# The SSD branch in two halves of its channels over four column tiles, and at most one side task begun per step

## The chip, the cores and the metric

The kernel runs on one core of a Trainium2 chip. The metric is the device time of one execution in microseconds (us); the times are medians of several executions.

## The reference, cut to what matters

One layer of a hybrid encoder for two requests of 256 tokens each (512 tokens in all), model width 1024, fp32:

```
x = x + 0.5 * swiglu(rms_norm(x), ffn1)
u = rms_norm(x);  q_na, k_na, v_na, q_mem, z, xbc, dt, gates = split(u @ w_in)
o_na  = neighborhood_attention(q_na, k_na, v_na)         # 16 heads of 64
o_ssd = grouped_rms_norm(ssd(xbc, dt) * silu(z), 8)      # 2048 channels, 8 groups of 256
o_mem = memory_attention(q_mem, mem)                     # 4 heads of 256
merged = sigmoid(g_na) * (o_na @ w_br_na) + sigmoid(g_ssd) * (o_ssd @ w_br_ssd) + sigmoid(g_mem) * (o_mem @ w_br_mem)
x = x + merged @ w_out
x = x + 0.5 * swiglu(rms_norm(x), ffn2)
```

The product `o_ssd @ w_br_ssd` has 2048 input channels (16 tiles of 128) and 1024 output channels (8 column tiles of 128).

## The kernel before

**Arithmetic.** Every product is made of three fp32r matmuls: each operand x is split into a high part (a cast to fp32r) and a low part (x minus the high part), and high x high, high x low and low x high are summed. So a weight tile `wr` of 128 x 1024 costs a cast `wh` on ScalarE (line 320) and a subtraction `wl` on VectorE (line 234), and an activation tile costs the same pair (`split_tile`: `osh`/`osl` for the SSD output, `mhh`/`mhl` for the merged one).

**The plan.** `make_plan` writes the whole layer as one list of units: the first FFN, the memory's keys and values, the projections for the attentions, the gates and branches of the memory attention, then for each of 8 SSD groups four convolution units and two z units with a gate or branch unit of the neighbourhood attention between them, then the 8 gate units of the SSD branch (`gate`, `ssd`, j), its 8 branch units (`br`, `ssd`, j), 8 units of the output projection (`wo`), and the second FFN. A unit of a gate has 8 x 3 matmuls of 512 columns; a unit of the SSD branch has 16 x 3, from two weight tiles of 8 channel tiles each, into one PSUM bank.

**Order around a unit.** `run` calls the unit's `do_` function (its matmuls), then `evacuate` (the evacuation of the unit before), then `step` (one step of the side tasks; after a gate of the SSD branch a second one). The evacuation of gate j is a tanh on ScalarE from the bank to a tile `tg`; that of branch j multiplies `tg` with the bank and adds it to `merged[j]`, which is then split.

**Side tasks.** What stands beside the matrix products (norms, attention, scans) is written as Python generators, put into a queue by `later` and advanced one yield per `step`. `step` advances every active task once, in order, and then begins tasks from the head of the queue; a task begins only when those it needs are done and not in the slot in which it was queued. Up to `width` tasks are active (3; 4 from the first gate of the SSD branch on), and the loop gives as many chances to begin one as `width`. `require` runs steps until given tasks are done. The ones that matter here:

- `na(p)`, p = 0 to 7 (`t_na`, 6 steps): a pair of heads of the neighbourhood attention. Step 1 issues 8 loads `nv<-scr_v` and the bias `bi<-in_strip` on SP and transposes the queries; step 2 transposes the keys and adds a mask to the bias on VectorE; step 3 makes the scores `ns` in two banks, adds the bias to them (`nt`), takes maxima and exponentials; then come the normalisation, the transposes and the output.
- `ssd(g)`, g = 0 to 7 (`t_ssd`, 14 steps): the scan of group g, with rows `rw<-scr_r` loaded on SP, matmuls `y`, and at the end the norm: a `sum` on PE, a chain of small VectorE operations, a diagonal `dg`, and `R` on PE, which spreads the norm. Groups 0 to 5 are parked in memory (`scr_o`, `scr_n`); 6 and 7 stay in SBUF (tiles `cv`).
- `os(g)` (`t_os`, one step): two tiles of the branch's input each. For g < 6 the norm (`rw<-scr_n`) and the tiles (`or<-scr_o`) are loaded on SP; each is scaled and split into `osh` and `osl`. `os(0)` to `os(3)` are queued at gate 0, `os(4)` to `os(7)` at the start of the branch, which requires all eight.

**Buffers.** Activations come from two pools, `pg` (54 tiles: u, cv, tg, mg, or, osh, osl, x, ...) and `pt` (21 tiles for temporaries: rw, e, nv, bi, ...). Weight tiles have a ring of 9, their split parts one of 3. PSUM has 5 banks for units (`m`, `q`, `ac`) and 3 for side tasks and the down projection. The order in which an engine gets its instructions is made by a scheduler at compile time: it goes by program order as a priority and by its own estimate of when inputs and buffers are there, so the queues differ from program order.

Of the kernel before, what the change touches and what calls it, by code (L numbers as in the profile page):

```python
# [10 lines left out]
ALU = mybir.AluOpType  # L11
# [5 lines left out]
KD = 8  # L17
# [24 lines left out]
def add_item(*args, **kw):  # L42
    ITEMS.append(Item(*args, **kw))
    return len(ITEMS) - 1


def plain(mat, k0, nk, col, m):
    n = f"c{len(ITEMS)}"
    return add_item(n, nk, m, [(n, (mat, k0, nk, col, m))])


def seven(p, key, block, nh):

    out = []
    for h in range(nh):
        n = lambda b: f"gu{key}.{h}.{b}"  # L60
        blk = lambda b: block(int(b[1]) - 1, int(b[2]) - 1, h)
        loads, src, sums = {1: (["B11"], "B11", []), 2: (["B21"], "B21", []), 5: (["B12"], "B11", [("B11", "B12")]),
                            6: (["B22"], "B11", [("B11", "B22")]), 3: ([], "B22", []), 7: ([], "B12", [("B12", "B22")]),
                            4: (["B21."], "B11", [("B11", "B21.")])}[p]
        _, _, nk, _, m = blk("B11")
        it = add_item(n(src), nk, m, [(n(b), blk(b)) for b in loads], [tuple(n(b) for b in t) for t in sums])
        out.append(("gu", (*key, p, h, nh), [it]))
    return out


def make_plan():

    s = []

    def a(kind, key, mat, col, ks=((0, 8),), m=128):
        s.append((kind, key, [plain(mat, k0, nk, col, m) for k0, nk in ks]))

    def quad(kind, q, mat, col):
        for c in range(4):
            s.append((kind, (q, c), [plain(mat, 2 * c, 2, col, 512)]))  # L80

    def ffn(f):

        before = None
        for ci, (c0, w) in enumerate(CBLOCKS + ((DFF, 0),)):
            n, down = w // 256, list(range(4)) if before else []

            def next_down():
                if down:
                    mp = down.pop(0)
                    s.append(("d", (f, ci - 1, mp), [plain(f + "_w_down", before[0], before[1], 256 * mp, 256)]))

            def part(p, ci=ci, c0=c0, w=w, n=n):
                s.extend(seven(p, (f, ci), lambda i, j, h: (f + ("_w_up", "_w_gate")[j], 4 * i + 4 // n * h, 4 // n, c0, w), n))

            if f == "ffn1" and ci == 0:
                for j, mat in enumerate(("_w_up", "_w_gate")):  # L100
                    for c in range(4):
                        s.append(("pl", (f, j, c), [plain(f + mat, 2 * c, 2, c0, w)]))
            else:
                for p in PRODUCTS if w else ():
                    if p == 4 and ci == 0:
                        rest = part
                        continue
                    part(p)
                    if p == 1 and ci == 1 and f == "ffn2":
                        rest(4)  # L110
                    if p in ((5, 6, 3, 7) if n == 2 else (5, 3, 7, 4)):
                        next_down()
            for _ in range(4):
                next_down()
            before = (c0 // 128, w // 128)

    def gate(br, j):
        a("gate", (br, j), "w_in", COL_G + 1024 * ("na", "ssd", "mem").index(br) + 128 * j)

    def branch(br, j):  # L120
        a("br", (br, j), "w_br_" + br, 128 * j, ks=((0, 8), (8, 8)) if br == "ssd" else ((0, 8),))

    ffn("ffn1")
    quad("km", 0, "w_mem_kv", 0)
    quad("km", 1, "w_mem_kv", 512)
    quad("vm", 0, "w_mem_kv", 1024)
    quad("vm", 1, "w_mem_kv", 1536)
    a("dt", 0, "w_in", COL_DT, m=64)
    quad("qm", 0, "w_in", COL_QM)
    quad("qm", 1, "w_in", COL_QM + 512)  # L130
    quad("v", 0, "w_in", COL_V)
    quad("v", 1, "w_in", COL_V + 512)
    for hf in range(2):
        quad("q", hf, "w_in", 512 * hf)
        quad("k", hf, "w_in", 1024 + 512 * hf)
    for j in range(8):
        gate("mem", j)
        branch("mem", j)
    light = [(f, j) for j in range(8) for f in (gate, branch)]
    for g in range(8):  # L140
        for i, (ct, col) in enumerate(((16 + g, COL_B + 128 * g), (24 + g, COL_C + 128 * g), (2 * g, COL_X + 256 * g),
                                       (2 * g + 1, COL_X + 256 * g + 128))):
            a("conv", (g, ct), "w_in", col)
            if i in (2, 3) and light:
                f, j = light.pop(0)
                f("na", j)
        a("z", (g, 0), "w_in", COL_Z + 256 * g)
        a("z", (g, 1), "w_in", COL_Z + 256 * g + 128)
    for j in range(8):
        gate("ssd", j)  # L150
    for j in range(8):
        branch("ssd", j)
    for m in (0, 4, 1, 5, 2, 6, 3, 7):
        a("wo", m, "w_out", m * 128)
    ffn("ffn2")
    return s


PLAN = make_plan()
CHUNKS = list(dict.fromkeys(c for it in ITEMS for _, c in it.loads))  # L160
OFFS = dict(zip(CHUNKS, np.concatenate([[0], np.cumsum([128 * nk * m for _, _, nk, _, m in CHUNKS])]).tolist()))
# [17 lines left out]
KEEP, EARLY, PG, LEND = 6, 4, 54, 4  # L179
# [3 lines left out]
class Layer:  # L183
# [145 lines left out]

    def step(self):  # L330

        for item in list(self.active) + [None] * self.width:
            if item is None:
                if len(self.active) >= self.width or not self.queue:
                    return
                _, _, need, born = self.queue[0]
                if born == self.n_slot or not all(k in self.done for k in need):
                    return
                item = self.queue.popleft()
                self.active.append(item)  # L340
            try:
                next(item[1])
            except StopIteration:
                self.done.add(item[0])
                self.active.remove(item)
# [692 lines left out]
    def pre_br(self, key):  # L1038
        br, j = key
        if j:  # L1040
            return
        if br == "mem":
            self.require(*[("am", h, b) for h in range(4) for b in range(2)])
            self.xo = [self.o.pop(("om", k)) for k in range(8)]
        elif br == "na":
            self.require(*[("na", p) for p in range(8)])
            self.xo = [self.o.pop(("on", k)) for k in range(8)]
        else:
            self.evacuate()
            self.u = None  # L1050
            for g in range(EARLY, 8):
                self.later(("os", g), self.t_os(g), (("ssd", g),))
            self.require(*[("os", g) for g in range(8)])
            self.xo = [self.os[k] for k in range(16)]

    def do_br(self, key, cis):
        br, j = key
        if key == ("ssd", 4):
            self.x = []
            for k in range(KD):  # L1060
                t = self.g(p="x2")
                self.nc.sync.dma_start(out=t, in_=self.scr_x[k])
                self.x.append(t)
        ps = self.unit(cis, self.xo)

        def evac():
            t = self.o.pop(("gate", br, j))
            if br == "mem":
                self.merged[j] = self.g(p="mg")
                self.stt(self.merged[j], t, 1.0, ps, ALU.add, ALU.mult)  # L1070
                return
            self.stt(t, t, 1.0, ps, ALU.add, ALU.mult)
            m = self.merged[j]
            self.tt(m, m, t, ALU.add)
            if key == ("na", 7):
                self.lent = 0
            if br == "ssd":
                self.merged[j] = self.split_tile(m, "mh")
        return evac

    def pre_wo(self, m):
# [335 lines left out]
```

## Time and profile before

| | |
|---|---|
| time, median of 3 runs | 1767.65 us (1766.73 to 1767.78) |
| the profiled execution | 1768.09 us, its span 1766.3 us |
| PE busy | 1741.1 us (99%) |
| VectorE (DVE) busy | 1232.2 us (70%) |
| ScalarE (ACT) busy | 847.3 us (48%) |
| mean granted TensorE clock | 0.994 |
| SSD branch, first to last matmul | about 1285.5 to 1373 us of the span |

PE is the TensorE, PEld its weight loads, SP the engine whose queue issues the DMAs. The granted clock is 1.00 at the higher of TensorE's two levels (2.4 GHz) and 0.50 at the lower (1.2 GHz). A matmul's duration overlaps the next one's; the distance of two starts tells what one costs.

### The profile page before, as it was taken

Reading aid. Unit: us, or ns where it says so; the run is one execution under the profiler, and the core shown is the slowest. Engines: PE = TensorE matmul, PEld = TensorE weight load, DVE = VectorE, ACT = ScalarE, POOL = GpSimd, SP = SyncE. Lnnn points to the kernel's source line nnn. Section 1 sums busy time; section 2 is a strip of 40 time slices with the busy share of each in tenths; the row PEclk is TensorE's granted clock in tenths of the full one; section 3 lists DMA queues with packets and bytes.
Section 4 is the critical chain, followed back from the end, with each engine's and each line's share of the span. In section 5 each row is a group of like instructions: output and inputs, shape, how many; then the busy total and the mean of one; then the engine's idle time right before and its main releaser. Section 6 shows DMA issues by size and latency. Waiting matters only on the chain.

```text
span 1766.3 us, 22623 instructions
## 1 busy us (share of the span) xinstructions
PE 1741.1 (99%) x8568; PEld 1425.2 (81%) x8568; DVE 1232.2 (70%) x2056; ACT 847.3 (48%) x1515; POOL 0.7 (0%) x5
## 2 busy tenths in 40 slices
PE   9999999999999999999999999999799999999999
PEld 7888888888788878888877777777588878888887
DVE  7676776875544466735778888888653697776775
ACT  6444444553323335533666766666432464444442
POOL 0000000000000000000000000000000000000000
PEclk9999999999999999999999999999899999999999
DMA  7144324442323232333344545347344234244341
GB/s 258 62 137 144 107 96 137 158 151 86 97 74 114 78 114 66 120 96 96 119 128 130 127 141 137 116 143 188 121 130 133 83 98 140 84 145 130 96 120 48
DMA packets 79708, 209.69 MB, mean 119 GB/s; under 512 B 11120, under 2 KB 19696, under 8 KB 79600
## 3 DMA queue, kind: packets, MB, share of 16 engines
q1 hardware_dynamic: 79600, 208.26, 38.1%
q8 instruction: 67, 1.10, 0.3%
q14 instruction: 41, 0.34, 0.1%
HBM read 198.64 MB, written 9.58 MB: 118 GB/s over the span
## 4 chain that ended last, share of the span: by engine, by line
PE 95%; DVE 3%; DMA 1%; issue 0%; ACT 0%; DVEq 0%; SPq 0%; ACTq 0%
PE ac L565 20%; PE m L543 12%; PE m L544 12%; PE m L545 12%; PE q L587 5%; PE q L589 5%; PE q L588 5%; PE d L544 5%; PE d L545 5%; PE d L543 5%; PE y L1278 2%; PE hT L690 1%; PE CB L1228 1%; DVE wl L234 1%; PE amo L875 1%; PE am L847 1%
## 5 line engine op out<-in xcount | busy, mean ns | idle before, releaser
L320 ACT CAST wh<-wr 128x1024 fp32r<-128x1024 f32 (+1 forms) x357 | 371.3, 1040 | 700.6 <-PE m L544 173.0
L234 DVE TENSOR_TENSOR wl<-wr,wh 128x1024 fp32r<-128x1024 f32 (+1 forms) x357 | 431.6, 1209 | 274.8 <-ACT wh L320 269.9
L543 PE MATMUL m<-uh,wh 128*128 128x512 f32 (+1 forms) x584 | 235.1, 403 | 2.7 <-ACT tg L249 2.7
L565 PE MATMUL ac<-wh,sh 128*128 128x512 f32 (+1 forms) x616 | 229.3, 373 | 0.8 <-ACT wh L320 0.8
L544 PE MATMUL m<-ul,wh 128*128 128x512 f32 (+1 forms) x584 | 229.0, 392 | 0.0
L565 PE MATMUL ac<-wl,sh 128*128 128x512 f32 (+1 forms) x616 | 228.1, 370 | 0.7 <-DVE wl L234 0.7
L545 PE MATMUL m<-uh,wl 128*128 128x512 f32 (+1 forms) x584 | 228.7, 392 | 0.0
L565 PE MATMUL ac<-wh,sl 128*128 128x512 f32 (+1 forms) x616 | 228.1, 370 | 0.0
L544 PE MATMUL d<-hl,wh 128*128 128x512 f32 x352 | 137.3, 390 | 0.7 <-DVE hl L234 0.7
L543 PEld LDWEIGHTS m<-uh,wh 128*128 128x128 f32 (+1 forms) x584 | 109.7, 188 | 34.9 <-ACT wh L320 5.4
L543 PE MATMUL d<-hh,wh 128*128 128x512 f32 x352 | 137.4, 390 | 0.5 <-ACT hh L256 0.5
L545 PE MATMUL d<-hh,wl 128*128 128x512 f32 x352 | 137.0, 389 | 0.0
L565 PEld LDWEIGHTS ac<-wh,sh 128*128 128x128 f32 x616 | 116.0, 188 | 21.0 <-ACT wh L320 1.7
L565 PEld LDWEIGHTS ac<-wl,sh 128*128 128x128 f32 x616 | 116.1, 188 | 20.6 <-DVE wl L234 1.2
L565 PEld LDWEIGHTS ac<-wh,sl 128*128 128x128 f32 x616 | 116.1, 188 | 19.6
L545 PEld LDWEIGHTS m<-uh,wl 128*128 128x128 f32 (+1 forms) x584 | 109.6, 188 | 25.2 <-issue 0.8
L544 PEld LDWEIGHTS m<-ul,wh 128*128 128x128 f32 (+1 forms) x584 | 109.8, 188 | 22.5 <-issue 0.4
L245 DVE SCALAR_TENSOR_TENSOR x<-d,x 128x512 f32<-128x512 f32 x96 | 66.2, 690 | 75.9 <-PE d L545 75.4
L587 PE MATMUL q<-wh,uh 128*128 128x512 f32 x256 | 103.0, 402 | 0.0
L234 DVE TENSOR_TENSOR wr<-wr,wr 128x1024 f32<-128x1024 f32 x80 | 97.6, 1221 | 7.1 <-DMA wr<-in_w 6.1
L588 PE MATMUL q<-wh,ul 128*128 128x512 f32 x256 | 100.7, 393 | 0.0
L589 PE MATMUL q<-wl,uh 128*128 128x512 f32 x256 | 100.6, 393 | 0.0
(253 smaller groups left out, 2856.5 us busy)
## 6 DMA issues: line engine op xcount, KB each, us to landing
wr<-in_w SPq DMA_DIRECT2D x308, 512.0 KB
rw<-scr_r SPq DMA_DIRECT2D x64, 256.0 KB
nv<-scr_v SPq DMA_DIRECT2D x64, 64.0 KB
scr_o<-cv SPq DMA_DIRECT2D x12, 256.0 KB
or<-scr_o SPq DMA_DIRECT2D x12, 256.0 KB
wr<-in_w SPq DMA_DIRECT2D x9, 256.0 KB
x<-in_xT SPq DMA_DIRECT2D x8, 256.0 KB
mr<-in_memT SPq DMA_DIRECT2D x8, 256.0 KB
```

Of the source, the lines that this page charges most:

```text
L234: self.V.tensor_tensor(out=out, in0=a, in1=b, op=op)
L245: self.V.scalar_tensor_tensor(out=out, in0=a, scalar=s, in1=b, op0=op0, op1=op1)
L320: self.S.copy(hi[:, :n], t[:, :n])
L543: self.T.matmul(ps[:m], wh[:, kk, :], xh, start=i == 0, stop=False)
L544: self.T.matmul(ps[:m], wh[:, kk, :], xl, start=False, stop=False)
L545: self.T.matmul(ps[:m], wl[:, kk, :], xh, start=False, stop=i == n - 1)
L565: go = lambda l, r, **f: self.T.matmul(ps, l, r, skip_group_check=True, **f)
L587: self.T.matmul(self.qb[t], xh, wh[:, kk, :], start=k == 0, stop=False)
L588: self.T.matmul(self.qb[t], xl, wh[:, kk, :], start=False, stop=False)
L589: self.T.matmul(self.qb[t], xh, wl[:, kk, :], start=False, stop=k == KD - 1)
L690: self.T.transpose(ps[:, (2 * r + t) * 128:(2 * r + t + 1) * 128], o["sg", r, t][:, c * 128:(c + 1) * 128], self.ident)
L1278: T.matmul(yb[64 * hp:64 * hp + 64, b * 256:(b + 1) * 256], xt[i][:, (2 * b + st) * 128 + 64 * hp:(2 * b + st) * 128 + 64 * hp + 64], w[hp ...
```

## The change

It does two things. First, the SSD branch is no longer 8 units of 16 channel tiles but 16 units `bs` of 8: for column tiles 0 to 3 the first 8 channel tiles, then for the same four the other 8, then the same for column tiles 4 to 7. Four banks are open at once. Only `os(0)` to `os(3)` are required before the first of them, `os(4)` to `os(7)` (still queued at the start of the branch) before the first second half. x is loaded back at unit (4, 0), where it was at branch 4. Second, `step` gives one chance to begin a task instead of `width`.

```diff
     def branch(br, j):
-        a("br", (br, j), "w_br_" + br, 128 * j, ks=((0, 8), (8, 8)) if br == "ssd" else ((0, 8),))
+        a("br", (br, j), "w_br_" + br, 128 * j)
...
-    for j in range(8):
-        branch("ssd", j)
+    for j0 in (0, 4):
+        for hf in range(2):
+            for j in range(j0, j0 + 4):
+                s.append(("bs", (j, hf), [plain("w_br_ssd", 8 * hf, 8, 128 * j, 128)]))
...
     def step(self):
 
-        for item in list(self.active) + [None] * self.width:
+        for item in list(self.active) + [None]:
...
+    def do_bs(self, key, cis):
+
+        j, hf = key
+        if key == (0, 0):
+            self.evacuate()
+            self.u = self.xo = None
+            for g in range(EARLY, 8):
+                self.later(("os", g), self.t_os(g), (("ssd", g),))
+            self.bs = {}
+        if j == 0:
+            self.require(*[("os", g) for g in range(4 * hf, 4 * hf + 4)])
+        if key == (4, 0):
+            self.x = []
+            for k in range(KD):
+                t = self.g(p="x2")
+                self.nc.sync.dma_start(out=t, in_=self.scr_x[k])
+                self.x.append(t)
+        if hf == 0:
+            self.bs[j] = self.bank()
+        ps = self.bs[j]
+        ci, = cis
+        self.ahead(ci)
+        wh, wl = self.split.pop(ci)
+        for kk in range(8):
+            xh, xl = self.os[8 * hf + kk]
+            k = 8 * hf + kk
+            go = lambda l, r, **f: self.T.matmul(ps, l, r, skip_group_check=True, **f)
+            go(wh[:, kk, :], xh, start=k == 0, stop=False)
+            go(wh[:, kk, :], xl, start=False, stop=False)
+            go(wl[:, kk, :], xh, start=False, stop=k == 15)
+        if hf == 0:
+            return None
+
+        def evac():
+            t, ps, m = self.o.pop(("gate", "ssd", j)), self.bs.pop(j), self.merged[j]
+            self.stt(t, t, 1.0, ps, ALU.add, ALU.mult)
+            self.tt(m, m, t, ALU.add)
+            self.merged[j] = self.split_tile(m, "mh")
+        return evac
```

The parts of `pre_br` and `do_br` for the SSD branch, which did the same for whole units, are removed.

## Rows read from the trace of the kernel before

**Rows 1.** The page: busy time by engine, and the clock in 40 slices.

```profile
PE 1741.1 (99%) x8568; PEld 1425.2 (81%) x8568; DVE 1232.2 (70%) x2056; ACT 847.3 (48%) x1515; POOL 0.7 (0%) x5
...
PEclk9999999999999999999999999999899999999999
```

**Rows 2.** Windows: stretch, length, busy time and instructions by engine, clock, DMA.

```profile
655.00:670.00 15.00, 11.70 (x114) 9.34 (x113) 12.27 (x31) 9.78 (x45) 0.00 (x0) 0.77 0.19 62
...
1256.00:1277.00 21.00, 10.57 (x39) 8.05 (x39) 11.49 (x28) 5.96 (x10) 0.00 (x0) 0.67 0.32 101
1285.50:1373.00 87.50, 87.50 (x386) 71.79 (x385) 40.65 (x49) 25.92 (x32) 0.00 (x0) 1.00 0.41 132
```

**Rows 3.** Timeline of PE at the gates: start, duration, instruction [idle before <-releaser].

```profile
1227.02 0.95 PE L504 MATMUL sum<-consts,yq 128*128 128x1 f32 x8
...
1234.55 1.05 PE L521 MATMUL R<-dg,consts 128*128 128x128 f32 x8
...
1262.69 1.70 PE L504 MATMUL sum<-consts,yq 128*128 128x1 f32 x8 [4.10 <-DVE yq L234]
1268.06 2.05 PE L521 MATMUL R<-dg,consts 128*128 128x128 f32 x8 [3.68 <-DVE dg L512]
1272.76 0.80 PE L543 MATMUL m<-uh,wh 128*128 128x512 f32 x1 [2.65 <-ACT tg L249]
...
1276.65 0.40 PE L543 MATMUL m<-uh,wh 128*128 128x512 f32 x1
```

**Rows 4.** Timeline of ScalarE at the gates and the branch's start.

```profile
1271.59 0.62 ACT L256 CAST osh<-or 128x512 fp32r<-128x512 f32 x1 [4.68 <-DVE or L245]
1272.12 2.54 ACT L249 ACTIVATE tg<-m 128x512 f32<-128x512 f32 x5
...
1302.09 2.18 ACT L256 CAST osh<-cv 128x512 fp32r<-128x512 f32 x4
```

**Rows 5.** Timeline of VectorE at the gates and the branch.

```profile
1232.51 0.69 DVE L234 TENSOR_TENSOR osl<-or,osh 128x512 fp32r<-128x512 f32 x1
...
1236.57 1.40 DVE L245 SCALAR_TENSOR_TENSOR cv<-cv,half,R 128x512 f32<-128x512 f32 x2
...
1249.76 0.69 DVE L234 TENSOR_TENSOR osl<-or,osh 128x512 fp32r<-128x512 f32 x1
...
1302.82 2.49 DVE L234 TENSOR_TENSOR osl<-cv,osh 128x512 fp32r<-128x512 f32 x4
1308.36 0.69 DVE L245 SCALAR_TENSOR_TENSOR tg<-tg,m 128x512 f32<-128x512 f32 x1 [3.04 <-PE m L545]
...
1311.53 0.69 DVE L245 SCALAR_TENSOR_TENSOR tg<-tg,m 128x512 f32<-128x512 f32 x1
```

**Rows 6.** SP's own waits, 1180 to 1320 us: total, times, longest.

```profile
SPq L288 <- DVE wl L234: 105.0, 18, 19.0
```

**Rows 7.** Timeline of SP's queue at the attention's start.

```profile
652.80 0.33 SPq L945 DMA_DIRECT2D bi<-in_strip  x1
```

**Rows 8.** Timeline of VectorE at the attention's start.

```profile
650.20 0.76 DVE L234 TENSOR_TENSOR bi<-bi,consts 128x256 f32<-128x256 f32 x2 [4.70 <-DMA bi<-in_strip]
...
657.44 0.76 DVE L234 TENSOR_TENSOR bi<-bi,consts 128x256 f32<-128x256 f32 x2 [3.96 <-DMA bi<-in_strip]
...
659.85 1.28 DVE L245 SCALAR_TENSOR_TENSOR nt<-ns,bi 128x512 f32<-128x512 f32 x2
```

**Rows 9.** Timeline of PE in the attention.

```profile
660.59 1.72 PE L979 MATMUL ns<-kT,qbd 64*64 64x128 f32 x32 [3.13 <-DVE nt L245]
...
725.84 1.60 PE L979 MATMUL ns<-kT,qbd 64*64 64x128 f32 x32 [0.85 <-DVE on L234]
```

**Rows 10.** Timeline of SP's queue at the gates.

```profile
1233.06 0.85 SPq L1316 DMA_DIRECT2D rw<-scr_n  x2
1233.96 0.90 SPq L1202 DMA_DIRECT2D rw<-scr_r  x2
...
1262.28 1.03 SPq L1316 DMA_DIRECT2D rw<-scr_n  x2
```

More of the change, by code (lines that the diff above doesn't have):

```diff
@@ L1044, in pre_br @@
             self.xo = [self.o.pop(("om", k)) for k in range(8)]
-        elif br == "na":
+        else:
             self.require(*[("na", p) for p in range(8)])
             self.xo = [self.o.pop(("on", k)) for k in range(8)]
[L1048 to L1054, printed above, removed]
     def do_br(self, key, cis):
         br, j = key
[L1058 to L1063, printed above, removed]
         ps = self.unit(cis, self.xo)
@@ L1076, in evac @@
                 self.lent = 0
-            if br == "ssd":
-                self.merged[j] = self.split_tile(m, "mh")
+        return evac
[35 more added lines that the diff above has]
+            self.merged[j] = self.split_tile(m, "mh")
         return evac
```

## The prediction

> **What bounds the kernel now.** The page comes first: TensorE (PE) is busy 1741.1 of 1766.3 us [rows 1]. Nothing that leaves PE's work and its waits alone can shorten this kernel. So a change has at most 25.2 us of PE idle to win, plus what PE loses to a lower clock. The strip of granted clock over 40 slices dips once, in the 31st [rows 1]. The windows, taken there and at every stretch where PE is not full, show two holes: 1256 to 1277 us and 655 to 670 us [rows 2]. The rest of PE's idle is scraps of under 1 us, the start and the tail.
>
> *The hole at the gates, 14.0 us.* Idle is 21.00 - 10.57 = 10.43 us, which the timeline of PE splits into 4.10, 3.68 and 2.65 [rows 2, 3]. The mean granted clock is 0.67: after it had stood idle, PE ran at the lower of its two levels (1.2 GHz). So nine matmuls take 3.9 us (1272.76 to 1276.65) instead of 9 x 0.227 = 2.0, the eight records of the sum 1.70 instead of 0.95 and those of R 2.05 instead of 1.05 [rows 3]: 3.6 us.
>
> Who is late? The last wait says it: PE waits for the tanh of a gate (tg) on ScalarE, and five of these stand in one row at 1272.12, right behind the last cast osh of the first four SSD groups [rows 3, 4]. Eight gate units run there, and the pool of matmul banks has five. Gates 1 to 5 had filled all five, so gate 6 could not start, and PE had nothing to put between the steps of the side task ssd(7). Tanh 1 had its input long before. What it lacked was a buffer for tg. The rows show that the pool pg gives buffers out in program order: the casts osh from cv stand at 1302.09, straight behind the last one from or, though two of these four cv tiles were scaled at 1236.57 and ScalarE had idled, 4.68 us before a single cast [rows 4, 5]. In program order the tasks os(0) to os(3) all stand in the first step after gate 1, before tanh 1, and their eight tiles come 5.75 us apart: (1249.76 - 1232.51) / 3 [rows 5]. Each load stands in SP's queue behind a weight load that waits for its ring buffer, 105.0 us in all in that stretch [rows 6].
>
> *The hole in the attention, 6.7 us.* Idle is 15.00 - 11.70 = 3.3 us, and the mean clock of 0.77 costs (1 - 0.77) x 15 = 3.4 more, since PE was busy while it was low [rows 2]. Three tasks na are begun in one step, so 27 loads enter SP's queue together; the third's bias is issued at 652.80 [rows 7]. VectorE stands at the bias of the second and third for 4.70 and 3.96 us, and the first's scores, which would free the score banks for PE, are read only behind that, at 659.85 [rows 8]. PE waits 3.13 us for it [rows 9].
>
> **The change part by part.**
>
> *Halves.* Matmuls (16 units x 24 = 384, as 8 x 48), weight loads (16), evacuations (8) and their operations stay the same in number. The branch fills 87.50 us, PE is busy 87.50 of them with 386 records, 0.227 us each, at clock 1.00 [rows 2]: there is no wait to remove. The scheduler that orders each engine's queue already does here what the halves do: the first two units are evacuated at 1308.36 and 1311.53 us [rows 5], 3.2 us apart although a unit takes 48 x 0.227 = 10.9, so their first halves ran early and together. Value: 0. No gain is possible; a loss needs late tiles of os(4) to os(7). They are done at 1302.82 + 2.49 = 1305.3, which is 19.8 us after the branch starts [rows 2, 5]. Four first halves cover 4 x 5.44 = 21.8 us; without that cover PE would wait for the rest. x comes back at the same place, half way, in eight loads on SP as before; the last of them may wait for an os buffer, and nothing reads that tile before the last output tile: 0. The removed require moves os(4), os(5), os(6) behind units (1,0), (2,0), (3,0) and os(7) to the start of (0,1). But the scheduler runs ahead of the program where a buffer is free: rw of os(4) was issued at 1262.28, 23 us before its place [rows 10]. So the end stays near +20: 0.
>
> *One begin per step.* I counted the queue through by hand, from the yields of each task: in 11 steps of the kernel before, more than one task begins. Three change nothing that PE waits for: two at the start (the squares end some three steps later, still three units before they are required) and one at the start of the second FFN. Three are those of the memory attention, where PE shows no wait: 0. The one at the branch is costed above. Three of the neighbourhood attention and one at the gates are left.
>
> Attention: na(0), na(1), na(2) now begin one unit of 24 x 0.227 = 5.44 us apart. The first's scores then stand ahead of the second's bias on VectorE, and a step asks for two score banks, not six. The bias of the later tasks is still somewhat late, since SP issues as many loads, but only VectorE waits, under PE's weight tiles split ahead. Bounds: 0 (the stall stays) to 6.7. For the leftover I take a place where only two tasks had begun together: PE idle 0.85 us at 725.84 [rows 9], with some clock 1.2. **-5.5 us.**
>
> Gates: os(0) and os(1) now stand behind gate 1, os(2) and os(3) behind gate 2, so tanh 1 gets its buffer after the fourth tile (1249.76 [rows 5]), not the eighth. Its bank is free before gate 5 ends (1262.69 - 4.10 = 1258.6 [rows 3]), and gate 6 fills 24 x 0.227 = 5.44 us in which PE was idle. Tanh 2 to 5 stay behind the eighth tile at 1272, and gate 7 starts there: the wait is shorter, not gone. Bounds: 0, if the eighth tile comes one gate later as its place does, to 14.0, if the tiles come faster. For the latter speaks that rw of os(2) and os(3) no longer take temporaries ahead of ssd(7)'s rows (1233.06 before 1233.96 [rows 10]). I take the mechanism between, **-5.4 us**.
>
> Sum: 1768.09 (the profiled execution: span 1766.3 and 1.8 around it) - 5.5 - 5.4 = 1757.2. That execution lies 0.4 above the median of the runs, so **1757 us**.
>
> **The rivals.**
>
> *Both holes close.* 1767.65 - 14.0 - 6.7 - 0.9 for the scrap at 726 us = 1746. For it: ssd(7) gets its rows earlier and may end under gate 6. Against: eight tiles at 5.75 us still need 40 us from the first to the last, and gates 2 to 5 wait for them.
>
> *Only the attention gains.* The chain of os tiles ends a gate later and eats what tanh 1 gives: 1767.65 - 5.5 = 1762.
>
> *The change does nothing.* The scheduler orders by its own estimate of times; if it packs the staggered tasks together again, the waits stay: 1768, within 0.2% (3.5 us, about what can be told from no change).
>
> *Slower: os(2) and os(3) come late.* Their loads now stand behind the weight loads of gate 2 and perhaps 3, and SP has waited up to 19.0 us for one ring buffer [rows 6]. Each us that the eighth tile comes later moves gate 7. Later by 16.4 us (three gates), the gates lose 16.4 - 5.4 = 11.0, and with the attention's 5.5 the time is 1773. It decides from 10.9 us on. Against it: the tiles came at an even 5.75 us, so no single wait of SP had held them that long.
>
> *Clock lost to the banks' turns.* At 0.43 us, as the nine slow ones ran, 384 matmuls would cost 78 us more; six times nine at that level, 1.85 us each, would cost 11 and bring the time back to 1768. The trace speaks against it: on five banks, with two units interleaved, the granted clock of the branch is 1.00 [rows 2]. The Trainium skill has a rule of this kind (TensorE: Matmul & The Clock Gate, "A second HAM failure mode: psum-queue depth-cycling"): cycling through PSUM banks makes PE idle briefly between groups of matmuls, and its clock swings between the two levels. By that rule the halves, which hold four banks open at once, would lose time in the branch; the 87.50 us at full clock contradict it here.
>
> **How the numbers follow.** Both holes shrink, 1750 to 1761: 0.60. Both close, 1743 to 1750: 0.10. Only the attention gains, 1761 to 1764: 0.12. Nothing, 1764 to 1771: 0.11. Late os: 0.05. Clock: 0.02, counted as slower at its upper end. Faster is 0.60 + 0.10 + 0.12 = 0.82, same 0.11, slower 0.07. The range 1746 to 1765 holds the first and the third, half of the second and a quarter of the fourth: 0.80.
>
> **What would show it.** Attention: the scores of one task per unit, no PE idle over 1 us at 655 to 670, clock 1.00. Gates: one tg at about 1250 us, between the fourth and the fifth osh, then four or five in a row; PE's wait before gate 7, not gate 6; the stretch from the first gate to the first branch matmul shorter by 5 us. Branch: 87 us as before, PE full. I would be wrong if tanh 1 stays behind all eight casts, if a wait for osh or osl appears at the first second half, or if PE waits for a bias again.

## The result and the profile after

The changed kernel takes 1756.6 us (median of 4 runs, 1756.35 to 1756.83); the kernel before took 1767.72 us beside it (4 runs). The ratio is 0.9937, with a 95% interval of 0.9919 to 0.9954: 11 us faster, at a forecast of 1757. The span of the profiled execution fell from 1766.3 to 1754.9 us.

The page of the changed kernel, in the lines that answer to [rows 1]:

```profile
PE 1737.2 (99%) x8568; PEld 1419.9 (81%) x8568; DVE 1234.6 (70%) x2056; ACT 848.0 (48%) x1515; POOL 0.7 (0%) x5
...
PEclk9999999999999999999999999999999999999999
```

PE's work is the same 8568 matmuls, its busy time 3.9 us less, since fewer ran at the low clock. The dip of the 31st slice is gone from the strip, but a slice is 44 us long and a shorter dip can hide in one. So the windows come next. They are the stretches of [rows 2], the second and third shifted by what the kernel had gained by then:

```profile
655.00:670.00 15.00, 14.31 (x124) 11.44 (x116) 12.46 (x31) 9.51 (x36) 0.00 (x0) 1.00 0.34 109
1253.00:1274.00 21.00, 13.80 (x61) 10.92 (x60) 11.37 (x27) 6.59 (x11) 0.00 (x0) 0.84 0.36 114
1274.85:1362.40 87.55, 87.55 (x388) 72.47 (x387) 40.77 (x50) 26.53 (x33) 0.00 (x0) 1.00 0.40 130
```

In the attention PE idles 0.69 us in place of 3.3 and its granted clock is 1.00 in place of 0.77. At the gates 7.20 us of idle stay of 10.43, at a mean clock of 0.84. The branch is full at clock 1.00, as before, with four banks open at once.

The timeline of PE, with the waits of the attention and the gates, to hold against [rows 3, 9]:

```profile
657.54 0.66 PE L951 MATMUL qT<-consts,qr 128*128 128x128 f32 x4 [0.69 <-DVE nt L247]
...
1221.99 0.94 PE L506 MATMUL sum<-consts,yq 128*128 128x1 f32 x8
...
1255.72 1.02 PE L506 MATMUL sum<-consts,yq 128*128 128x1 f32 x8
...
1259.87 1.13 PE L523 MATMUL R<-dg,consts 128*128 128x128 f32 x8 [0.48 <-DVE dg L514]
1267.72 0.79 PE L545 MATMUL m<-uh,wh 128*128 128x512 f32 x1 [6.72 <-ACT tg L251]
...
1271.26 0.39 PE L547 MATMUL m<-uh,wl 128*128 128x512 f32 x1
...
1361.92 0.39 PE L545 MATMUL m<-mhh,wh 128*128 128x512 f32 x1
```

Three waits at the gates have become one of 6.72 us before gate 7 and one of 0.48. The second sum now runs in between the matmuls of gate 6, with no wait; R follows right behind them. The timeline of ScalarE says why the wait before gate 7 is there:

```profile
1244.23 0.60 ACT L258 CAST osh<-or 128x512 fp32r<-128x512 f32 x1
1246.07 0.59 ACT L251 ACTIVATE tg<-m 128x512 f32<-128x512 f32 x1
1249.19 0.62 ACT L258 CAST osh<-or 128x512 fp32r<-128x512 f32 x1 [2.53 <-DVE or L247]
...
1266.56 0.62 ACT L258 CAST osh<-or 128x512 fp32r<-128x512 f32 x1 [3.74 <-DVE or L247]
1267.08 2.54 ACT L251 ACTIVATE tg<-m 128x512 f32<-128x512 f32 x5
```

One tanh, that of gate 1, stands between the fourth and the fifth cast; the next five stand in one row behind the eighth.

**Where the time came from.** The same instruction in both traces tells it: one at the first FFN's end, the branch's first matmul and the first product behind the branch. Timelines of PE, first of the kernel before, then of the changed one (its `m<-mhh` stands above):

```profile
350.71 0.50 PE L543 MATMUL d<-hh,wh 128*128 128x512 f32 x1 [0.24 <-ACT hh L256]
...
1285.50 0.39 PE L543 MATMUL m<-osh,wh 128*128 128x512 f32 x1
...
1372.99 0.39 PE L543 MATMUL m<-mhh,wh 128*128 128x512 f32 x1
```

```profile
351.15 0.50 PE L545 MATMUL d<-hh,wh 128*128 128x512 f32 x1 [0.24 <-ACT hh L258]
...
1274.88 0.39 PE L1094 MATMUL m<-osh,wh 128*128 128x512 f32 x1
```

At the first FFN's end, 350.71 before and 351.15 after, the changed kernel is 0.44 us late. At the first `sum` above, before the gates' holes, it is 1227.02 - 1221.99 = 5.03 us early: the stretch with the attention in it gave 5.5. At the branch's first matmul, 1285.50 before and 1274.88 after, it is 10.62 us early: the gates gave 5.6. At the first product behind the branch (`m<-mhh`), 1372.99 before and 1361.92 after, it is 11.07 us early: gates and branch together gave 6.0. At the last down projection, 1750.85 before and 1739.36 after, it is 11.49: 0.4 more from scraps in the second FFN.

The gain at the gates is not the idle time that went there, 10.43 - 7.20 = 3.2 us. PE goes on at a fixed distance behind the eighth cast: 1272.76 - 1271.59 = 1.17 us before, 1267.72 - 1266.56 = 1.16 after. What counts is how much work is left behind that point. One gate less is left, 24 x 0.227 = 5.44 us; the faster `sum` and `R` ahead of it only make the wait longer.

### The profile page after: what moved, and what is told of

Same layout as the page of the kernel before. It is cut to its first block, busy times and chain, and to the rows that moved or that the text cites. A ratio compares the mean times of both kernels' runs of the same rounds, so it can differ in the third digit from the quotient of the medians.

```text
span 1754.9 us, 22611 instructions
## 1 busy us (share of the span) xinstructions
PE 1737.2 (99%) x8568; PEld 1419.9 (81%) x8568; DVE 1234.6 (70%) x2056; ACT 848.0 (48%) x1515; POOL 0.7 (0%) x5
## 4 chain that ended last, share of the span: by engine, by line
PE 96%; DVE 2%; DMA 1%; ACT 1%; issue 0%; SPq 0%; DVEq 0%; ACTq 0%
PE ac L567 20%; PE m L545 10%; PE m L546 10%; PE m L547 10%; PE q L589 5%; PE q L591 5%; PE q L590 5%; PE m L1094 5%; PE d L546 5%; PE d L547 5%; PE d L545 5%; PE y L1305 2%; PE hT L692 1%; PE CB L1255 1%; PE q L609 1%; PE q L611 1%
```

## The experiments

Ten kernels were timed against the kernel before. Diffs are against the changed kernel or the kernel before, as said.

**Which of the two parts?** First the limit alone, in the kernel before:

```diff
-        for item in list(self.active) + [None] * self.width:
+        for item in list(self.active) + [None]:
```

> The limit of one begin per step alone, whole branch units kept. My theory (the halves are worth 0, both gains come from the limit): 1757 us like the changed kernel, -11, with one tg between the fourth and the fifth osh and no idle in the branch. Rival (the halves cover late os tiles): 3 us or more slower than the changed kernel, with PE waiting for osh or osl in the branch.

Measured: 1757.76 us (5 runs, 1756.53 to 1758.51), ratio 0.994 (0.9926 to 0.9953). Its timeline of PE has the wait of the changed kernel before gate 7:

```profile
1267.12 0.79 PE L543 MATMUL m<-uh,wh 128*128 128x512 f32 x1 [6.75 <-ACT tg L249]
```

Then the halves alone, the changed kernel with the old line of `step`:

```diff
-        for item in list(self.active) + [None]:
+        for item in list(self.active) + [None] * self.width:
```

> The halves alone, with as many begins per step as before. My theory: 1768 us, no change beyond 0.2%, both holes of PE as before (14 us at the gates, 6.7 in the attention). Rival (the halves gain something): 1764 us or less, with a shorter stretch from the first gate to the output projection.

Measured: 1768.08 us (11 runs), ratio 0.9999 (0.999 to 1.0008). Its windows show both holes as in [rows 2], and the branch full:

```profile
655.00:670.00 15.00, 11.73 (x115) 9.69 (x114) 11.86 (x29) 9.50 (x43) 0.00 (x0) 0.77 0.22 70
1256.00:1277.00 21.00, 10.58 (x40) 8.01 (x39) 10.92 (x28) 5.96 (x10) 0.00 (x0) 0.67 0.31 101
1285.00:1372.00 87.00, 87.00 (x386) 72.03 (x385) 40.49 (x49) 25.98 (x33) 0.00 (x0) 1.00 0.41 131
```

So the limit makes the whole of the difference that can be measured, and the halves make none. The 1.2 us between the limit alone and the changed kernel lie inside both intervals.

**Which of the places?** The number of active tasks, `width`, is 3 up to the gates of the SSD branch and 4 from there on, so the limit can be set on either side alone, in the changed kernel. Before the gates only:

```diff
-        for item in list(self.active) + [None]:
+        for item in list(self.active) + [None] * (1 if self.width == 3 else self.width):
```

> The changed kernel with the limit only before the first gate of the SSD branch; from there on as many begins as before. My theory (the two gains are separate and add): -5.5 us, 1762, attention hole closed, hole at the gates of 14 us back, PE waiting before gate 6. Rival (the attention's gain is lost on the way): 1767 or more.

Measured: 1762.87 us (5 runs), ratio 0.9969 (0.9957 to 0.9981). From the gates on only (`self.width == 4` in that line):

> The changed kernel with the limit only from the first gate of the SSD branch on. My theory: -5.5 us, 1762, attention hole of 6.7 us back, one tg between the fourth and the fifth osh at the gates, PE waiting before gate 7. Rival (the gates gain only because the attention ran earlier): 1767 or more.

Measured: 1762.11 us (4 runs), ratio 0.9965 (0.9951 to 0.9978). Timelines of PE, first of the limit before the gates, then of the limit from the gates on:

```profile
657.37 0.66 PE L951 MATMUL qT<-consts,qr 128*128 128x128 f32 x4 [0.69 <-DVE nt L247]
...
1258.03 1.83 PE L506 MATMUL sum<-consts,yq 128*128 128x1 f32 x8 [4.10 <-DVE yq L236]
...
1268.24 0.80 PE L545 MATMUL m<-uh,wh 128*128 128x512 f32 x1 [2.65 <-ACT tg L251]
```

```profile
661.98 4.74 PE L981 MATMUL ns<-kT,qbd 64*64 64x128 f32 x50 [4.53 <-DVE nt L247]
...
1266.99 1.13 PE L523 MATMUL R<-dg,consts 128*128 128x128 f32 x8 [0.49 <-DVE dg L514]
...
1274.75 0.80 PE L545 MATMUL m<-uh,wh 128*128 128x512 f32 x1 [6.63 <-ACT tg L251]
```

Each side closes its own hole and leaves the other. The gains are 1767.89 - 1762.87 = 5.0 and 1767.89 - 1762.11 = 5.8 us (1767.89 is the kernel before beside these runs); together 10.8, beside 10.1 for the limit alone and 11.1 for the changed kernel. The hole that is left is not always the same size: in the profiled execution of the limit from the gates on, PE's wait in the attention is 4.53 us, where [rows 9] have 3.13, and its first `sum` comes 2.1 us later than before (1229.10 after 1227.02). So a difference of 1 or 2 us in this hole between single profiles shows little.

**Is it buffers that hold the tanh?** In the kernel before, with all its begins, the tanh tiles get a pool of their own, of eight tiles that are taken from `pg`. Sizes and work stay the same; only the order in which buffers are given out differs:

```diff
-KEEP, EARLY, PG, LEND = 6, 4, 54, 4
+KEEP, EARLY, PG, LEND = 6, 4, 46, 4
...
+        self.ptg = pool("ptg", 8)
...
-        pl = self.pt if p in TEMPS else self.pg
+        pl = self.ptg if p == "tg" else self.pt if p in TEMPS else self.pg
```

> The kernel before, with the eight tanh tiles tg in a pool of their own (8 tiles, pg cut from 54 to 46), nothing else changed. My theory (the buffer in program order is what tanh 1 to 5 lack): each tanh comes soon after its gate, PE does not wait before gate 6, the hole at the gates falls from 14 to under 4 us: 1754 us, if 46 tiles do elsewhere. Rival (the step's program order puts the casts ahead on ScalarE, buffers or not): five tanh in one row after the last cast, and 1768 or more.

Measured: 1753.51 us (4 runs, 1753.32 to 1755.06), ratio 0.9916 (0.9901 to 0.9931). Its timelines, first of ScalarE at gates 1 and 2, then of PE in the attention:

```profile
1229.52 0.58 ACT L250 ACTIVATE tg<-m 128x512 f32<-128x512 f32 x1
1230.63 0.62 ACT L257 CAST osh<-or 128x512 fp32r<-128x512 f32 x1 [0.53 <-DVE or L246]
1233.95 0.59 ACT L250 ACTIVATE tg<-m 128x512 f32<-128x512 f32 x1
1236.30 0.62 ACT L257 CAST osh<-or 128x512 fp32r<-128x512 f32 x1 [1.36 <-DVE or L246]
```

```profile
660.54 4.18 PE L980 MATMUL ns<-kT,qbd 64*64 64x128 f32 x50 [3.28 <-DVE nt L246]
```

The tanh of gates 1 and 2 stand ahead of casts that they stood behind in [rows 4]; PE waits at the gates for nothing longer than 0.3 us, and the hole of the attention is as it was. The gain of 1768.48 - 1753.51 = 15.0 us is the 14.0 of the gates' hole and 1.0 more, inside the interval (12.2 to 17.5); the spans differ by 1766.3 - 1751.8 = 14.5.

**Is it the bias that holds the scores?** In the kernel before, `t_na` loads the bias ahead of its eight `nv` loads; the same nine loads, in another order on SP:

```diff
+        bias = self.g(p="bi")
+        self.nc.sync.dma_start(out=bias, in_=self.a["strip"][pr])
         for b in range(2):
...
-        bias = self.g(p="bi")
-        self.nc.sync.dma_start(out=bias, in_=self.a["strip"][pr])
```

> The kernel before, with the bias of each na task loaded ahead of its eight nv loads instead of behind them; three tasks still begin in one step. My theory (VectorE standing at a late bias makes the hole): its waits of 4.70 and 3.96 us shrink to under 1, the hole in the attention from 6.7 to under 2 us: 1763 us. Rival (three tasks in step ask for six score banks of three, whatever the bias does): hole and time as before, 1768.

Measured: 1762.39 us (5 runs, 1761.79 to 1764.17), ratio 0.9967 (0.9954 to 0.998). Timelines of VectorE and PE, to hold against [rows 8, 9], and the window:

```profile
652.05 0.75 DVE L234 TENSOR_TENSOR bi<-bi,consts 128x256 f32<-128x256 f32 x2
...
656.96 1.23 DVE L234 TENSOR_TENSOR wl<-wr,wh 128x1024 fp32r<-128x1024 f32 x1 [1.52 <-ACT wh L320]
658.10 1.28 DVE L245 SCALAR_TENSOR_TENSOR nt<-ns,bi 128x512 f32<-128x512 f32 x2
```

```profile
658.84 1.68 PE L979 MATMUL ns<-kT,qbd 64*64 64x128 f32 x32 [0.88 <-DVE nt L245]
...
660.72 1.42 PE L979 MATMUL ns<-kT,qbd 64*64 64x128 f32 x18 [0.20 <-DVE nt L245]
```

```profile
655.00:670.00 15.00, 13.91 (x130) 11.21 (x129) 12.21 (x35) 11.52 (x51) 0.00 (x0) 0.89 0.32 93
```

The third bias is added at 652.05, not 657.44, and VectorE waits for none of it. Three tasks are still begun in one step, but PE's wait is 1.08 us in place of 3.3. By the window 6.7 - 1.1 of idle - 1.7 of clock ((1 - 0.89) x 15) = 3.9 us are won, and the spans say the same: 1766.3 - 1762.4 = 3.9. The runs give 6.1, between 3.5 and 8.1; the profiled execution is the longest of the five (1764.17; the others take 1761.79 to 1762.56). So the larger part of the hole was the bias, late among 27 loads on SP. In the profile 2.8 us are left while three tasks begin in one step. By the runs nothing is: moving the bias gave 6.1 us, the limit before the gates 5.0, and their intervals overlap. So it is not shown that three begins cost anything beside the late bias. If they do, this trace points at neither the score banks nor the loads: the first scores are read (658.10) right behind a weight split `wl`, for which VectorE had waited 1.52 us for ScalarE's cast. That is read from one profile and not tested.

**Can the rest of the gates' hole be had?** `run` calls `step` a second time after each gate of the SSD branch, so one begin per step still means two os tasks per gate. In the changed kernel the second step is let begin none:

```diff
-    def step(self):
+    def step(self, begin=True):
...
-        for item in list(self.active) + [None]:
+        for item in list(self.active) + [None] * begin:
...
             if kind == "gate" and key[0] == "ssd":
-                self.step()
+                self.step(False)
```

> The changed kernel, and the second step after a gate begins no task, so os(0) to os(3) stand behind gates 1, 2, 3, 4 with a tanh between each two. My theory (tg waits for its buffer behind the os tiles in program order): tanh 1 after the second tile, tanh 2 after the fourth, tanh 3 after the sixth; gate 7 no longer waits; the hole of 6.72 us idle and some 1.6 us of low clock goes: 1748 us. Rival (ScalarE takes the casts first whatever the buffers, or the eighth tile just comes later): the tanh stay in one row behind the last cast and the time stays at 1756 or rises.

Measured: 1747.37 us (4 runs, 1746.54 to 1747.87), ratio 0.9878 (0.9861 to 0.9894): 21 us faster than the kernel before, 9 to 10 faster than the changed one (1756.6 - 1747.4 by the medians, 0.9937 - 0.9878 by the ratios). Timeline of ScalarE at the gates, and windows from the gates into the branch:

```profile
1233.71 0.57 ACT L251 ACTIVATE tg<-m 128x512 f32<-128x512 f32 x1
...
1245.01 0.58 ACT L251 ACTIVATE tg<-m 128x512 f32<-128x512 f32 x1
...
1256.70 0.59 ACT L251 ACTIVATE tg<-m 128x512 f32<-128x512 f32 x1
...
1267.00 0.62 ACT L258 CAST osh<-or 128x512 fp32r<-128x512 f32 x1
1267.52 2.05 ACT L251 ACTIVATE tg<-m 128x512 f32<-128x512 f32 x4
```

```profile
1215.00:1262.00 47.00, 47.00 (x226) 34.96 (x225) 39.07 (x97) 29.70 (x60) 0.00 (x0) 1.00 0.52 168
1265.00:1350.00 85.00, 85.00 (x376) 70.17 (x375) 40.28 (x50) 27.79 (x36) 0.00 (x0) 1.00 0.41 134
```

A tanh stands behind every second cast, and PE is full. The eighth cast is where it was (1267.00, after 1266.56): the os tiles come no sooner, but the first three tanh no longer stand behind all of them. Four tanh still wait behind it, and that costs nothing, since banks enough come free one by one.

The same with the bias first as well:

> Both: second step begins none, bias first, on the changed kernel. My theory: the attention of the changed kernel has only scraps left (0.69 and 0.68 us idle), so the bias adds at most 1 us to the gain of the second step: 1747 to 1748 us. Rival (the later bias of the staggered tasks still costs PE): 1745 or less.

Measured: 1747.32 us (4 runs), ratio 0.9879 (0.9865 to 0.9894): no more. Once the attention's tasks begin one unit apart, the order of their loads is worth nothing that the runs can tell.

The other remedy on top of the change, its tanh tiles in a pool of eight (edit as above):

> The changed kernel with the tanh tiles of the gates in a pool of eight of their own, taken from pg (54 to 46). If the 6.7 us that PE still waits before gate 7, and the clock behind it, come only from tanh tiles that wait for buffers behind the casts of os(2) and os(3), the wait goes: 1756.6 - 6.7 - 1.8 (eight matmuls at 0.43 to 0.45 us in place of 0.227) - some of the slow sums = 1747 to 1748, and each tanh stands soon after its gate. Rival: the wait before gate 7 is that of the os tiles themselves, through the smaller pool pg or the steps of ssd(7): then PE waits elsewhere in the gates or at the branch's start, and the time stays at 1753 or above.

Measured: 1747.66 us (4 runs, 1747.24 to 1748.65), ratio 0.9885 (0.9868 to 0.9901). Two different edits that both free the tanh end at the same time, with 47.00 of 47.00 us busy in the same window of PE.

**Do the halves matter where the gates end early?** The fastest version with the branch put back into whole units:

> The limit of one begin per step, none at all in the second step after a gate, and the branch in whole units as before: the halves are taken back out of the fastest version so far (1747.4). If the halves are worth nothing, as the other runs had it, the time is 1747 to 1748 and PE stands idle nowhere at the branch. Rival: the gates now end some 9 us earlier and the os tasks are begun one unit further apart, so that the tiles of os(4) to os(7) come too late for whole units, and the halves are what covers them here: then PE waits for osh or osl at the first branch units, for up to 8 us, and the time is 1750 to 1756.

Measured: 1747.38 us (4 runs, 1747.12 to 1748.13), ratio 0.9882 (0.9867 to 0.9897). Window of the branch and PE's one wait in it, then timelines of VectorE there, first of this kernel, then of the changed one:

```profile
1264.80:1352.60 87.80, 87.48 (x385) 71.76 (x384) 41.18 (x50) 27.92 (x36) 0.00 (x0) 1.00 0.41 132
```

```profile
1273.01 0.50 PE L543 MATMUL m<-osh,wh 128*128 128x512 f32 x1 [0.32 <-ACT osh L256]
```

```profile
1285.71 2.49 DVE L234 TENSOR_TENSOR osl<-cv,osh 128x512 fp32r<-128x512 f32 x4
1289.36 0.69 DVE L245 SCALAR_TENSOR_TENSOR tg<-tg,m 128x512 f32<-128x512 f32 x1 [1.17 <-PE m L545]
1292.54 0.69 DVE L245 SCALAR_TENSOR_TENSOR tg<-tg,m 128x512 f32<-128x512 f32 x1
```

```profile
1294.05 2.49 DVE L236 TENSOR_TENSOR osl<-cv,osh 128x512 fp32r<-128x512 f32 x4
...
1302.29 0.69 DVE L247 SCALAR_TENSOR_TENSOR tg<-tg,m 128x512 f32<-128x512 f32 x1 [3.31 <-PE m L1094]
...
1307.72 0.69 DVE L247 SCALAR_TENSOR_TENSOR tg<-tg,m 128x512 f32<-128x512 f32 x1 [2.29 <-PE m L1094]
```

With whole units the first evacuations are 3.2 us apart, as in [rows 5], where one unit's matmuls take 10.9: the scheduler interleaves them by itself. With halves they are 5.4 apart, one second half after the other. The rival's wait for `osh` is there in whole units, but it is 0.32 us and not up to 8; in the changed kernel PE does not wait in the branch. The last tiles are done 1285.71 + 2.49 - 1264.82 = 23.4 us after this kernel's first branch matmul, and 21.7 us (1294.05 + 2.49 - 1274.88) after it in the changed one.

## Why the prediction was right, point by point

**The limit alone pays.** Forecast: halves 0, attention -5.5, gates -5.4. Measured by position in the trace: attention -5.5, gates and branch -6.0; by runs: halves 0, the limit before the gates 5.0, from the gates on 5.8. The tail's 0.4 and the start's 0.44 were not forecast, and cancel.

**Attention.** The cause that was read out of [rows 7, 8], a bias late among 27 loads and ahead of the scores on VectorE's queue, is shown by the run that moves the bias alone: with three begins as they were, 3.9 us of the 6.7 go by its profile and 6.1 by the runs (3.5 to 8.1). The other part that the prediction had named without a price of its own, six score banks asked for in one step, is not shown to cost anything. The leftover, taken as 1.2 from a place with two tasks, is 0.69 of idle and no clock at this place. That 1.2 was 0.85 of idle and 0.35 for the clock, and the 0.35 stood in no row; the window around that place in the kernel before has clock 1.00:

```profile
720.00:730.00 10.00, 9.15 (x122) 7.31 (x121) 7.66 (x14) 4.28 (x16) 0.00 (x0) 1.00 0.44 129
```

So by its own window the attention gave 6.7 - 0.7 = 6.0, and half a microsecond was lost again between there and the gates, where the traces show no one place for it. That forecast and position agree on 5.5 to the tenth is luck.

**Gates.** The steps came as named: tanh 1 after the fourth cast, at 1246.07; gate 6's matmuls ahead of the eighth cast, priced at 5.44 and measured as 5.6 up to the branch; the wait before gate 7, on five tanh behind the eighth cast. The eighth cast came 1271.59 - 1266.56 = 5.03 us earlier, exactly the shift that the kernel had at the first `sum`, so its distance from there did not change, neither for better nor for worse. That decided between the rivals: the one in which os(2) and os(3) come late needed that cast to move back, the one in which both holes close needed it to move forward or the tanh not to hang on it. One argument for the latter did come true, and was not enough: ssd(7) ended under gate 6, with 0.48 us of wait left of 4.10 and 3.68, but gate 7 hung on the tanh.

**Buffers in program order.** This was read from casts that stood in a row although the inputs of some had long been there. That buffers are what the tanh lacked is now shown by the pool of their own, which removes the whole hole with every begin as it was, and the rest of it on top of the change. It also sizes the hole: put at 14.0 us, it gave 15.0 in the runs and 14.5 in the spans. Perfetto Trace Analysis, in the Trainium skill, says under "Optimization Strategy" that the same gap repeating on the engine that should be full can mean that no SBUF or PSUM is there for the next tile. Here the trace agrees that PE stood idle for want of a buffer, but the gaps were three in one place and the count of buffers was the same in both versions, 54 and 46 + 8; only who waits behind whom was changed.

**Halves.** The worth of 0 came out, by the halves alone (0.9999) and without them in the fastest version. The prediction took 4 x 5.44 = 21.8 us as what four first halves cover. That bound was too tight: in the changed kernel with no begin in the second step the last tiles are done 27.1 us after the branch's first matmul (1290.63 + 2.49 - 1266.02), and PE waits for none.

**Clock.** The rival in which four open banks cost clock did not come: 1.00 over the 87.55 us of the branch, and a ratio of 0.9999 for the halves alone. The rule named there, of the Trainium skill's TensorE: Matmul & The Clock Gate ("A second HAM failure mode: psum-queue depth-cycling"), does not show in this kernel, where no PE idle stands between the groups.

What stays open: why the scraps in the second FFN are 0.4 us shorter, and the 0.44 us at the start; both are under what the runs can tell.

## What to carry to other kernels

Where several late-starting tasks draw on one pool of buffers, a short task queued behind them waits for theirs even when its own input is long there; look for instructions that stand in a row at the moment another's last tile is done, and give the short one its own few buffers, or begin the others later. Here the own buffers alone were worth 15 us, the change 11, and both together 21. A matrix branch that PE already runs without a gap gains nothing from being cut into halves; what has to be found first is the idle time, not the loop that looks too long.

## What the runs showed of the hardware that was not expected

After the one wait of 6.72 us PE's next eight matmuls took 1271.26 - 1267.72 = 3.54 us in place of 8 x 0.227 = 1.82, and then it was back at 0.227: 1.7 us lost to the clock behind one wait, where three waits of 10.43 us in all had lost 3.6. In the attention a wait of 0.69 us left the clock of the window at 1.00 in the changed kernel, and two of 0.88 and 0.20 came with 0.89 in the kernel with the bias first: at about a microsecond of idle, the price in clock was nothing in one kernel and 1.7 us, more than the idle itself, in the other. What PE ran around these waits differs too: 96 score matmuls of 64 rows between 656.00 and 662.1 with the bias first, 32 of them at a time in the changed kernel. Which of the two the clock answered to, no run tells apart.
